# Stick-breaking heads with queries as rows and a scan over later keys

## The chip, the cores and the metric

The kernel runs on one core of one Trainium2 chip. The metric is device time in microseconds (us). Before the change three runs took 1114.95, 1115.48 and 1116.98 us, median 1115.48. One further execution was taken with the profiler; the profile and the trace below are of that one.

## The reference

The reference is a decoder of two layers, 512 tokens of width 1024 in fp32. Layer 0 has latent attention and differential attention, layer 1 has dilated attention and stick-breaking attention; a gated feed-forward part with a short convolution follows each. The change touches the four stick-breaking heads alone. For one head of width 64, with queries q, keys k and values v:

```python
strict = kpos[None, :] < qpos[:, None]
z = jnp.einsum('bhqd,bhkd->bhqk', qblk, k).astype(jnp.float32) * scale
log_beta = jax.nn.log_sigmoid(z)
log_keep = jnp.where(strict, jax.nn.log_sigmoid(-z), 0.0)
after = lax.cumsum(log_keep, axis=3, reverse=True) - log_keep
a = jnp.where(strict, jnp.exp(log_beta + after), 0.0)
return jnp.einsum('bhqk,bhkd->bhqd', a.astype(v.dtype), v)
```

With softplus(z) = log(1 + exp(z)), log_sigmoid(z) = z - softplus(z) and log_sigmoid(-z) = -softplus(z). So the weight of a key is exp(z - the sum of softplus over this key and all later keys in front of the query). That sum along the keys is what the change computes in another way.

## The kernel before, in words

TensorE does nearly all products of the layer's projections as three products each (`mm3`, L554 to L556): an fp32 operand is split into a part that is rounded to fp32r and its rest, and high times high, high times low and low times high are summed in PSUM. `split` (L461) makes the rounded part on ACT (L462) and the rest on DVE (L463). Weights go the same way: `Weights.load` brings a block of 128x1024 on SP's queue (L292) into one of three raw buffers, ACT casts it (L314), DVE makes the rest (L315), and up to five pairs are kept ahead of their use.

In the function `odd` (second layer) the token activations stand as `xh`, `xl`. `proj_T` computes a transposed projection of 128 columns by 512 tokens: 24 products into a bank named `apt`, which ACT (L1918) or DVE (L1920) then copies out. `proj_V` does the values by token blocks (`apv`, 24 narrower products for each block of 128 tokens), copied out to `sv` by ACT or DVE. Names of the PSUM banks used here: tag `a` has three banks, `s` two, `t`, `o` and `n` one each.

Four stick-breaking heads are worked as two pairs, u = 0 and u = 1; the heads of a pair lie in partitions 0 to 63 and 64 to 127 of `sq[u]` and `sk[u]`. Tokens are taken in four blocks of 128. Before the change a head's scores stand with keys as rows (partitions) and queries as columns: for key block j the queries from block j on, so 512 + 384 + 256 + 128 = 1280 columns, at the offsets `off`. For each pair:

- `sb_scores`: eight products (L1983) into `zp`, the two heads side by side; DVE adds the causal mask and writes `z` (L1987); DVE caps at 40 into `sp` (L1993); ACT takes exp (L1994).
- `sb_softplus`: ACT takes log of 1 + that (L1999), DVE takes the maximum with `z` (L2000). ACT loads its function table anew when it goes from exp to log and back.
- `sb_weights`: `sp` is split into `sh` (ACT) and `sl` (DVE). The sum over later keys runs over partitions, so TensorE does it: products with `tri`, whose first half holds -1 where a key is not earlier and whose second half is -1 throughout, add up the blocks j2 from j on, twice each (L2014, 20 products of 128 to 512 columns for each head, into `cp`). DVE adds `cp` to `z` (L2017), ACT takes exp of all 1280 columns (L2018).
- `sb_values`: eight products of `sv` with the weights, four for each head, into `osb` (L2024); `split` makes `oS` of it.

Between these steps stand eight `proj_T` for the dilated heads (`T12`), four for each pair, as work for TensorE while the other engines run. The order here is not written out by hand: the recorded order of the calls is passed to a list scheduler, which places instructions on each engine by its own costs. What follows (`score12`, first product L2090, and later) is again in hand-written order.

`store_sums(1, True)` (L426) has GpSimd's DMA queue add up some of the feed-forward weights in memory for later. Its first transfer is tied to the last DVE instruction that was written ahead of it.

Of the kernel before, what the change touches and what calls it, by code (L numbers as in the profile page):

```python
# [11 lines left out]
F32 = mybir.dt.float32  # L12
F32R = mybir.dt.float32r
BF16 = mybir.dt.bfloat16
AF = mybir.ActivationFunctionType
# [4 lines left out]
P = 128  # L20
# [329 lines left out]
def trunk(tc, A, out):  # L350
# [3 lines left out]
    with ExitStack() as top:  # L354
# [1529 lines left out]
        def odd(xnT, pending):  # L1884
            xh, xl = xnT
            with ExitStack() as es:
# [14 lines left out]
                                                                sb.tile([P, 2, S], F32, tag="sk", name="sk"))]  # L1901
                sv = sb.tile([P, NT, 256], F32, tag="sv", name="sv")
                smask = sb.tile([P, S], F32, tag="smask", name="smask")
                tri = sb.tile([P, 2, P], F32R, tag="tri", name="tri")
                trif = sb.tile([P, 2, P], F32, tag="z", name="trif", bufs=2)

                def proj_T(dst, scale, permuted, on_act):
                    acc = bank("a", "apt")
# [13 lines left out]
                def proj_V(dst, on_act=False):  # L1922
                    ws = [W.next() for _ in range(2)]

                    def tile_V(i):
                        t = slice(i * P, (i + 1) * P)
                        a = bank("a", "apv")
                        for k in range(KD):
                            wh, wl = ws[k // 4]
                            c = slice((k % 4) * 256, (k % 4 + 1) * 256)  # L1930
                            mm3(a[:, :256], xh[:, k, t], xl[:, k, t], wh[:, c], wl[:, c], k == 0, k == KD - 1)
                        if i % 2 and not on_act:
                            DVE.tensor_copy(dst[:, i], a[:, :256])
# [35 lines left out]
                tile_V = proj_V(sv)  # L1969
                for i in ORDER:  # L1970
                    tile_V(i)
                off = (0, 512, 896, 1152, 1280)
                spans = ((0, 0, 512), (1, 512, 896), (2, 896, 1280))

                def sb_scores(u):

                    zs = [sb.tile([P, 1280], F32, tag="z", name="z", bufs=2) for _ in range(2)]
                    for n, (j0, o0, o1) in enumerate(spans):
                        zp = [bank(t, "zp") for t in ("ss", "nt", "aa")[n]]
                        for j in (j0,) if j0 < 2 else (2, 3):  # L1980
                            for y in range(2):
                                r = slice(y * 64, y * 64 + 64)
                                PE.matmul(zp[y][:, off[j] - o0:off[j + 1] - o0], sk[u][r, j * P:(j + 1) * P],  # L1983
                                          sq[u][r, j * P:], start=True, stop=True)
                        for y in range(2):
                            for j in (j0,) if j0 < 2 else (2, 3):
                                DVE.tensor_tensor(zs[y][:, off[j]:off[j + 1]], zp[y][:, off[j] - o0:off[j + 1] - o0],  # L1987
                                                  smask[:, :S - j * P], ALU.add)

                    sps = []  # L1990
                    for z in zs:
                        sp = sb.tile([P, 1280], F32, tag="sp", name="sp", bufs=2)
                        DVE.tensor_scalar(sp[:], z[:], 40.0, None, ALU.min)  # L1993
                        ACT.activation(sp[:], sp[:], AF.Exp)  # L1994
                        sps.append(sp)
                    return list(zip(zs, sps))
# [3 lines left out]
                    DVE.tensor_tensor(sp[:], z[:], sp[:], ALU.max)  # L2000

                def sb_weights(z, sp):
                    sh = sb.tile([P, 1280], F32R, tag="sh", name="sh")
                    sl = sb.tile([P, 1280], F32R, tag="sl", name="sl")
                    split(sh[:], sl[:], sp[:])

                    for j0, o0, o1 in spans:
                        zp = bank("ssn"[j0], "cp")
                        for j in (j0,) if j0 < 2 else (2, 3):
                            n = S - j * P  # L2010
                            c = off[j] - o0
                            for j2 in range(j, NT):
                                for part in (sh, sl):
                                    PE.matmul(zp[:, c + (j2 - j) * P:c + n], tri[:, 0 if j2 == j else 1],  # L2014
                                              part[:, off[j2]:off[j2 + 1]], start=(j2 == j and part is sh),
                                              stop=(j2 == NT - 1 and part is sl))
                        DVE.tensor_tensor(z[:, o0:o1], z[:, o0:o1], zp[:, :o1 - o0], ALU.add)  # L2017
# [8 lines left out]

                T12 = [lambda t=t, x=x: proj_T(t[x], (-0.125, 1.0)[t is ck], True, t is cq)
                       for x in range(2, 6) for t in (cq, ck)]
                for u in range(2):
                    zs = sb_scores(u)  # L2030
                    for _ in range(2):
                        T12.pop(0)()
                    if u == 0:
                        with tc.manual_schedule(engines={POOL.engine}):
                            store_sums(1, True)
                    for v in zs:
                        sb_softplus(*v)
                    T12.pop(0)()
                    for v in zs:
                        sb_weights(*v)  # L2040
                    T12.pop(0)()
                    o = bank("o", "osb")
                    sb_values(u, [z for z, _ in zs], o)
# [276 lines left out]
def layout(inputs):  # L2320
# [76 lines left out]
    m = np.where(p < np.arange(P)[None, :], 0.0, -BIG)  # L2397
    o = np.zeros((P, P))
    r["sb_mask"] = np.concatenate([m, o, o, o], 1).astype(f)
    r["sb_tri"] = np.stack([-(p >= np.arange(P)[None, :]).astype(f), -np.ones((P, P), f)], 1)  # L2400
    return {k: np.ascontiguousarray(v) for k, v in r.items()}


# [13 lines left out]
```

## Time and profile before

| | before |
|---|---|
| median of three runs | 1115.48 us |
| profiled execution, its own time | 1116.25 us |
| its span, first to last instruction | 1114.5 us |
| PE (matmul) busy | 1104.3 us, 99% |
| DVE busy | 913.8 us, 82% |
| ACT busy | 638.6 us, 57% |
| granted TensorE clock, mean | 0.999 |

Engines are PE (TensorE's products), PEld (its weight loads), DVE (VectorE), ACT (ScalarE), POOL (GpSimd) and SP (SyncE, which here issues transfers). A row of a group names the line, the engine, the operation, output and inputs, the shape and the count, then the summed busy time and the mean of one in ns, then the idle time of the engine ahead of them with what ended it. A product that the program gives in fp32, as L1983 and L2024 are, appears as two records. The length of one product's record reaches beyond the start of the next, because products are pipelined; the time that a series takes is therefore read from start to start or from the chain of waits, which gives each piece's share of the path.

### The profile page before, as it was taken

Reading aid. Unit: us, or ns where it says so; the run is one execution under the profiler, and the core shown is the slowest. Engines: PE = TensorE matmul, PEld = TensorE weight load, DVE = VectorE, ACT = ScalarE, POOL = GpSimd, SP = SyncE. Lnnn points to the kernel's source line nnn. Section 1 sums busy time; section 2 is a strip of 40 time slices with the busy share of each in tenths; the row PEclk is TensorE's granted clock in tenths of the full one; section 3 lists DMA queues with packets and bytes.
Section 4 is the critical chain, followed back from the end, with each engine's and each line's share of the span. In section 5 each row is a group of like instructions: output and inputs, shape, how many; then the busy total and the mean of one; then the engine's idle time right before and its main releaser. Section 6 shows DMA issues by size and latency. Waiting matters only on the chain.

```text
span 1114.5 us, 17776 instructions
## 1 busy us (share of the span) xinstructions
PE 1104.3 (99%) x6556; PEld 951.7 (85%) x6556; DVE 913.8 (82%) x1628; ACT 638.6 (57%) x1127; POOL 219.1 (20%) x285
## 2 busy tenths in 40 slices
PE   9999999999999999999999999999999999999997
PEld 8766677898999999788888877788989999988886
DVE  5776687589999999999873565677899999999995
ACT  6554555447666666566553464654556676655662
POOL 2231022243022232000020030112521321220002
PEclk9999999999999999999999999999999999999999
DMA  8496122273444136455634295313534432265561
GB/s 309 161 216 109 54 95 96 76 248 124 152 137 157 42 101 251 137 174 178 233 110 169 78 244 132 97 53 112 192 129 154 144 123 76 78 250 180 159 213 76
DMA packets 53302, 162.14 MB, mean 145 GB/s; under 512 B 6720, under 2 KB 9184, under 8 KB 53216
## 3 DMA queue, kind: packets, MB, share of 16 engines
q1 hardware_dynamic: 45936, 145.22, 38.4%
q0 software_dynamic: 5312, 13.68, 6.4%
q10 hardware_dynamic: 1968, 2.12, 0.7%
q8 instruction: 51, 0.84, 0.3%
q14 instruction: 35, 0.29, 0.1%
HBM read 145.23 MB, written 27.28 MB: 155 GB/s over the span
## 4 chain that ended last, share of the span: by engine, by line
PE 92%; DVE 3%; DMA 2%; POOL 1%; issue 1%; ACT 0%; POOLq 0%; SPq 0%; DVEq 0%; ACTq 0%
PE u L554 13%; PE u L555 13%; PE u L556 13%; PE acc L555 6%; PE acc L556 6%; PE acc L554 6%; PE apt L554 3%; PE apt L555 3%; PE apt L556 3%; PE sps L1430 1%; PE ao L554 1%; PE ao L556 1%; PE ao L555 1%; PE aqk L1231 1%; PE aqk L1229 1%; PE aqk L1227 1%
## 5 line engine op out<-in xcount | busy, mean ns | idle before, releaser
L554 PE MATMUL u<-xh,wh 128*128 128x256 f32 (+1 forms) x664 | 212.3, 320 | 0.0
L555 PE MATMUL u<-xl,wh 128*128 128x256 f32 (+1 forms) x664 | 212.0, 319 | 0.0
L556 PE MATMUL u<-xh,wl 128*128 128x256 f32 (+1 forms) x664 | 211.6, 319 | 0.0
L732 DVE SCALAR_TENSOR_TENSOR y<-u,cw,y 128x511 f32<-128x511 f32 (+1 forms) x176 | 129.6, 746 | 9.2 <-ACT y L727 6.2
L315 DVE TENSOR_TENSOR wl<-wraw,wh 128x1024 fp32r<-128x1024 f32 x92 | 111.3, 1219 | 29.9 <-ACT wh L314 29.8
L556 PEld LDWEIGHTS u<-xh,wl 128*128 128x128 f32 x664 | 126.5, 190 | 9.0
L554 PEld LDWEIGHTS u<-xh,wh 128*128 128x128 f32 x664 | 126.6, 191 | 8.3
L555 PEld LDWEIGHTS u<-xl,wh 128*128 128x128 f32 x664 | 126.6, 191 | 8.0
L314 ACT CAST wh<-wraw 128x1024 fp32r<-128x1024 f32 x92 | 95.5, 1050 | 60.3 <-PE apt L555 18.0
L556 PE MATMUL u<-th,wl 128*128 128x256 f32 x416 | 117.7, 283 | 0.0
L555 PE MATMUL u<-tl,wh 128*128 128x256 f32 x416 | 117.7, 283 | 0.0
L554 PE MATMUL u<-th,wh 128*128 128x256 f32 x416 | 117.6, 283 | 0.0
L716 DVE TENSOR_TENSOR wl<-wraw,wh 128x512 fp32r<-128x512 f32 (+1 forms) x116 | 107.7, 938 | 2.2 <-ACT wh L864 1.5
L864 ACT CAST wh<-wraw 128x512 fp32r<-128x512 f32 (+1 forms) x104 | 86.5, 859 | 35.6 <-DVE wraw L851 23.0
L555 PE MATMUL acc<-wl,gh 128*128 128x512 f32 (+1 forms) x250 | 96.5, 389 | 0.1
L556 PE MATMUL acc<-wh,gl 128*128 128x512 f32 (+1 forms) x250 | 96.3, 388 | 0.0
L716 POOL TENSOR_TENSOR wl<-wraw,wh 128x512 fp32r<-128x512 f32 x48 | 62.3, 1298 | 172.0 <-issue 30.7
L554 PE MATMUL acc<-wh,gh 128*128 128x512 f32 (+1 forms) x250 | 93.6, 389 | 0.7 <-ACT wh L314 0.7
L727 ACT ACTIVATE y<-u,cw 128x512 f32<-128x512 f32 x88 | 67.5, 780 | 32.9 <-PE u L556 28.3
L554 PEld LDWEIGHTS u<-th,wh 128*128 128x128 f32 x416 | 79.8, 192 | 0.8
L555 PEld LDWEIGHTS u<-tl,wh 128*128 128x128 f32 x416 | 79.8, 192 | 0.7
L556 PEld LDWEIGHTS u<-th,wl 128*128 128x128 f32 x416 | 79.8, 192 | 0.0
(388 smaller groups left out, 2558.8 us busy)
## 6 DMA issues: line engine op xcount, KB each, us to landing
wraw<-in_ffn_w_up SPq DMA_DIRECT2D x82, 512.0 KB, 4.0
wraw<-in_ffn_w_down SPq DMA_DIRECT2D x44, 512.0 KB, 3.7
summed<-in_ffn_w_up POOLq DMA_DIRECT2D x24, 256.0 KB, 7.5
wraw<-summed SPq DMA_DIRECT2D x12, 512.0 KB, 4.2
wraw<-in_od_w_dqk SPq DMA_DIRECT2D x12, 512.0 KB, 3.9
wraw<-in_ffn_w_down SPq DMA_DIRECT2D x22, 256.0 KB, 3.2
wraw<-in_ev_w_dqk SPq DMA_DIRECT2D x8, 512.0 KB, 3.6
wraw<-in_ev_w_out SPq DMA_DIRECT2D x8, 512.0 KB, 3.6
```

What stands on the lines that cost most here:

```text
L314: self.nc.scalar.copy(h[:, :w], raw[:, :w])
L315: self.nc.vector.tensor_tensor(l[:, :w], raw[:, :w], h[:, :w].bitcast(F32), ALU.subtract)
L554: PE.matmul(o, lh, rh, start=first, stop=False, skip_group_check=more)
L555: PE.matmul(o, lh, rl, start=False, stop=False, skip_group_check=more)
L556: PE.matmul(o, ll, rh, start=False, stop=last, skip_group_check=more)
L716: return engine.tensor_tensor(o, a, b, ALU.subtract)
L727: ACT.activation(ys[n][:, z], us[n][z], AF.Identity, bias=cw[:, PAIRED[n], z, 3:4], scale=c[:, 2:3])
L732: DVE.scalar_tensor_tensor(y[:, z, d:], u[:, :S - d], c[:, 2 - d:3 - d], y[:, z, d:], ALU.mult, ALU.add)
L864: ACT.copy(ws[n][w][0][:, c], src)
L1227: PE.matmul(o, lh, rh, start=first, stop=False)
L1229: PE.matmul(o, lh, rl, start=False, stop=False)
L1231: PE.matmul(o, ll, rh, start=False, stop=last)
```

## The change

The heads' scores now stand with queries as rows and keys as columns: for query block i the keys up to block i, again 1280 columns in all, at the offsets `row`. The sum over later keys now runs along the columns, and DVE does it with a running scan: for each query block `tensor_tensor_scan` goes over the columns of `sp` from the last to the first (step -1), adds each to the sum so far, adds a zero (`none`, one column read again and again), and writes `kept` at the same reversed places. DVE subtracts `kept` from `z`. The value product needs keys as rows, so TensorE turns `z` block by block (ten transposes of 128x128 for each head, into `tz`), and ACT takes exp from the turned blocks in PSUM, three instructions in place of one, into `sp`. The triangle, its load and cast and the split of `sp` are gone. The mask is turned too.

The written order of the calls changes with it. The first pair's scores stand ahead of the value projection, which before stood in front of them. Of the eight projections in `T12`, two stand behind the first pair's softplus, one between its two heads' weights; then come the second pair's scores, ahead of the first pair's values; then two, one, one and one around the second pair's steps. `store_sums` is written behind the value projection.

```diff
-                tri = sb.tile([P, 2, P], F32R, tag="tri", name="tri")
-                trif = sb.tile([P, 2, P], F32, tag="z", name="trif", bufs=2)
+                none = sb.tile([P, 1], F32, tag="none", name="none")
...
-                nc.scalar.dma_start(trif[:], A["sb_tri"])
                 nc.scalar.dma_start(tab12[:], A["dil_tab12"])
-                DVE.tensor_copy(tri[:], trif[:])
+                DVE.memset(none[:], 0.0)
...
-                tile_V = proj_V(sv)
-                for i in ORDER:
-                    tile_V(i)
                 off = (0, 512, 896, 1152, 1280)
+                row = (0, 128, 384, 768, 1280)
...
-                    for n, (j0, o0, o1) in enumerate(spans):
+                    for n, at in enumerate((((3, 0),), ((2, 0), (0, 384)), ((1, 0),))):
                         zp = [bank(t, "zp") for t in ("ss", "nt", "aa")[n]]
-                        for j in (j0,) if j0 < 2 else (2, 3):
+                        for i, o in at:
                             for y in range(2):
                                 r = slice(y * 64, y * 64 + 64)
-                                PE.matmul(zp[y][:, off[j] - o0:off[j + 1] - o0], sk[u][r, j * P:(j + 1) * P],
-                                          sq[u][r, j * P:], start=True, stop=True)
+                                PE.matmul(zp[y][:, o:o + row[i + 1] - row[i]], sq[u][r, i * P:(i + 1) * P],
+                                          sk[u][r, :(i + 1) * P], start=True, stop=True)
...
                 def sb_weights(z, sp):
-                    sh = sb.tile([P, 1280], F32R, tag="sh", name="sh")
-                    sl = sb.tile([P, 1280], F32R, tag="sl", name="sl")
-                    split(sh[:], sl[:], sp[:])
+                    kept = sb.tile([P, 1280], F32, tag="sh", name="kept")
+                    for i in (3, 2, 1, 0):
+                        back = slice(row[i + 1] - 1, row[i] - 1 if i else None, -1)
+                        DVE.tensor_tensor_scan(kept[:, back], sp[:, back], none[:].to_broadcast([P, (i + 1) * P]), 0.0,
+                                               ALU.add, ALU.add)
+                    DVE.tensor_tensor(z[:], z[:], kept[:], ALU.subtract)
...
-                        zp = bank("ssn"[j0], "cp")
+                        tp = bank("ssn"[j0], "tz")
                         for j in (j0,) if j0 < 2 else (2, 3):
...
-                            for j2 in range(j, NT):
-                                for part in (sh, sl):
-                                    PE.matmul(zp[:, c + (j2 - j) * P:c + n], tri[:, 0 if j2 == j else 1],
-                                              part[:, off[j2]:off[j2 + 1]], start=(j2 == j and part is sh),
-                                              stop=(j2 == NT - 1 and part is sl))
-                        DVE.tensor_tensor(z[:, o0:o1], z[:, o0:o1], zp[:, :o1 - o0], ALU.add)
-                    ACT.activation(z[:], z[:], AF.Exp)
+                            for i in range(j, NT):
+                                c = off[j] - o0 + (i - j) * P
+                                PE.transpose(tp[:, c:c + P], z[:, row[i] + j * P:row[i] + (j + 1) * P], ident[:])
+                        ACT.activation(sp[:, o0:o1], tp[:, :o1 - o0], AF.Exp)
...
-                for u in range(2):
-                    zs = sb_scores(u)
...
+                def fill(n):
+                    for _ in range(n):
                         T12.pop(0)()
...
+                def finish(u, zs):
                     o = bank("o", "osb")
+                    sb_values(u, [sp for _, sp in zs], o)
                     split(oS[0][:, u], oS[1][:, u], o)
...
+                zs = sb_scores(0)
+                tile_V = proj_V(sv)
+                for i in ORDER:
+                    tile_V(i)
+                with tc.manual_schedule(engines={POOL.engine}):
+                    store_sums(1, True)
+                for v in zs:
+                    sb_softplus(*v)
+                fill(2)
+                sb_weights(*zs[0])
+                fill(1)
+                sb_weights(*zs[1])
+                first, zs = zs, sb_scores(1)
+                finish(0, first)
+                fill(2)
+                for v in zs:
+                    sb_softplus(*v)
+                fill(1)
+                sb_weights(*zs[0])
+                fill(1)
+                sb_weights(*zs[1])
+                fill(1)
+                finish(1, zs)
```

Line numbers of the changed kernel differ a little: there the scores are L1979, their mask L1983, the cap L1989, exp and log L1990 and L1995, the maximum L1996, the scan L2002 (listed as a scalar-tensor-tensor operation), the subtraction L2004, the transposes L2011, the exp L2012, the values L2018, the copies of a projection L1917 and L1919, those of `sv` L1932 and L1934, and the next part begins at L2099.

The order on PE in front of the last projections of the first pair, before (`apt` is a projection of `T12`, `cp` the sum over later keys, `sh` and `sl` the two parts of `sp`):

```order
L556 MATMUL apt<-xh,wl 128x512
L2014 MATMUL cp<-sh,tri 128x512
L2014 MATMUL cp<-sl,tri 128x512
L2014 MATMUL cp<-sh,tri 128x384
L2014 MATMUL cp<-sl,tri 128x384
L2014 MATMUL cp<-sh,tri 128x256
```

The same place on PE after the change (`tz` is the turned block):

```order
L556 MATMUL apt<-xh,wl 128x512
L2011 MATMUL tz<-ident,z 128x128 x10
L554 MATMUL apt<-xh,wh 128x512
L555 MATMUL apt<-xl,wh 128x512
L556 MATMUL apt<-xh,wl 128x512
```

The first five of a head's twenty products with the triangle are shown before; ten transposes in one series stand in their place, and the projections go on behind them.

PE where the second pair's scores are made, before, with buffer numbers (each number of `zp` is a bank; two numbers beside each other are the two heads):

```order
L2024 MATMUL osb_6748<-z_6497,sv_6027 64x128
L2024 MATMUL osb_6748<-z_6498,sv_6027 64x128
L1983 MATMUL zp_6761<-sq_6025,sk_6026 128x512
L1983 MATMUL zp_6762<-sq_6025,sk_6026 128x512
L1983 MATMUL zp_6767<-sq_6025,sk_6026 128x384
L1983 MATMUL zp_6768<-sq_6025,sk_6026 128x384
L1983 MATMUL zp_6773<-sq_6025,sk_6026 128x256
L1983 MATMUL zp_6774<-sq_6025,sk_6026 128x256
L1983 MATMUL zp_6773<-sq_6025,sk_6026 128x128
L1983 MATMUL zp_6774<-sq_6025,sk_6026 128x128
```

And after the change:

```order
L2011 MATMUL tz_6680<-ident_84,z_6380 128x128 x4
L2011 MATMUL tz_6686<-ident_84,z_6380 128x128 x3
L2011 MATMUL tz_6691<-ident_84,z_6380 128x128 x3
L1979 MATMUL zp_6705<-sk_6026,sq_6025 128x384
L1979 MATMUL zp_6705<-sk_6026,sq_6025 128x128
L1979 MATMUL zp_6698<-sk_6026,sq_6025 128x512
L1979 MATMUL zp_6699<-sk_6026,sq_6025 128x512
L1979 MATMUL zp_6704<-sk_6026,sq_6025 128x384
L1979 MATMUL zp_6704<-sk_6026,sq_6025 128x128
L1979 MATMUL zp_6714<-sk_6026,sq_6025 128x256
L1979 MATMUL zp_6715<-sk_6026,sq_6025 128x256
```

The scores stood behind the first pair's values (`osb`) and now stand ahead of them, directly behind the transposes of the first pair's second head. Banks 6698, 6699 and 6704 are those that `tz` 6680, 6686 and 6691 have just filled. The products of 384 and of 128 columns are no longer beside the other head's.

DVE in the second pair from the maximum on, before (`wl` is the rest of a weight block, `ck` a projection's copy):

```order
L2000 TENSOR_TENSOR sp<-z,sp 128x1280
L315 TENSOR_TENSOR wl<-wraw,wh 128x1024
L2000 TENSOR_TENSOR sp<-z,sp 128x1280
L463 TENSOR_TENSOR sl<-sp,sh 128x1280
L1920 TENSOR_SCALAR ck_6015<-apt 128x512
```

And after the change:

```order
L1996 TENSOR_TENSOR sp<-z,sp 128x1280
L1919 TENSOR_SCALAR ck_6014<-apt 128x512
L1996 TENSOR_TENSOR sp<-z,sp 128x1280
L315 TENSOR_TENSOR wl<-wraw,wh 128x1024
L2002 SCALAR_TENSOR_TENSOR kept<-sp,none 128x512
L2002 SCALAR_TENSOR_TENSOR kept<-sp,none 128x384
L2002 SCALAR_TENSOR_TENSOR kept<-sp,none 128x256
L2002 SCALAR_TENSOR_TENSOR kept<-sp,none 128x128
L2004 TENSOR_TENSOR z<-z,kept 128x1280
L315 TENSOR_TENSOR wl<-wraw,wh 128x1024
```

In place of the split stand four scans and a subtraction for the first head; the second head's follow the last row shown.

More of the change, by code (lines that the diff above doesn't have):

```diff
@@ L1977, in sb_scores @@
                     zs = [sb.tile([P, 1280], F32, tag="z", name="z", bufs=2) for _ in range(2)]
-                    for n, (j0, o0, o1) in enumerate(spans):
+                    for n, at in enumerate((((3, 0),), ((2, 0), (0, 384)), ((1, 0),))):
                         zp = [bank(t, "zp") for t in ("ss", "nt", "aa")[n]]
-                        for j in (j0,) if j0 < 2 else (2, 3):
+                        for i, o in at:
                             for y in range(2):
                                 r = slice(y * 64, y * 64 + 64)
-                                PE.matmul(zp[y][:, off[j] - o0:off[j + 1] - o0], sk[u][r, j * P:(j + 1) * P],
-                                          sq[u][r, j * P:], start=True, stop=True)
+                                PE.matmul(zp[y][:, o:o + row[i + 1] - row[i]], sq[u][r, i * P:(i + 1) * P],
+                                          sk[u][r, :(i + 1) * P], start=True, stop=True)
                         for y in range(2):
-                            for j in (j0,) if j0 < 2 else (2, 3):
-                                DVE.tensor_tensor(zs[y][:, off[j]:off[j + 1]], zp[y][:, off[j] - o0:off[j + 1] - o0],
-                                                  smask[:, :S - j * P], ALU.add)
+                            for i, o in at:
+                                DVE.tensor_tensor(zs[y][:, row[i]:row[i + 1]], zp[y][:, o:o + row[i + 1] - row[i]],
+                                                  smask[:, S - (i + 1) * P:], ALU.add)
                     sps = []
@@ L2002, in sb_weights @@
                 def sb_weights(z, sp):
-                    sh = sb.tile([P, 1280], F32R, tag="sh", name="sh")
-                    sl = sb.tile([P, 1280], F32R, tag="sl", name="sl")
-                    split(sh[:], sl[:], sp[:])
+                    kept = sb.tile([P, 1280], F32, tag="sh", name="kept")
[4 more added lines that the diff above has]
+                    DVE.tensor_tensor(z[:], z[:], kept[:], ALU.subtract)
                     for j0, o0, o1 in spans:
-                        zp = bank("ssn"[j0], "cp")
+                        tp = bank("ssn"[j0], "tz")
                         for j in (j0,) if j0 < 2 else (2, 3):
-                            n = S - j * P
-                            c = off[j] - o0
-                            for j2 in range(j, NT):
-                                for part in (sh, sl):
-                                    PE.matmul(zp[:, c + (j2 - j) * P:c + n], tri[:, 0 if j2 == j else 1],
-                                              part[:, off[j2]:off[j2 + 1]], start=(j2 == j and part is sh),
-                                              stop=(j2 == NT - 1 and part is sl))
-                        DVE.tensor_tensor(z[:, o0:o1], z[:, o0:o1], zp[:, :o1 - o0], ALU.add)
-                    ACT.activation(z[:], z[:], AF.Exp)
+                            for i in range(j, NT):
+                                c = off[j] - o0 + (i - j) * P
+                                PE.transpose(tp[:, c:c + P], z[:, row[i] + j * P:row[i] + (j + 1) * P], ident[:])
+                        ACT.activation(sp[:, o0:o1], tp[:, :o1 - o0], AF.Exp)
                 def sb_values(u, a, o):
@@ L2028, in odd @@
                        for x in range(2, 6) for t in (cq, ck)]
-                for u in range(2):
-                    zs = sb_scores(u)
-                    for _ in range(2):
+                def fill(n):
+                    for _ in range(n):
                         T12.pop(0)()
[L2033 to L2041, printed above, removed]
+                def finish(u, zs):
                     o = bank("o", "osb")
-                    sb_values(u, [z for z, _ in zs], o)
+                    sb_values(u, [sp for _, sp in zs], o)
                     split(oS[0][:, u], oS[1][:, u], o)
+                zs = sb_scores(0)
[21 more added lines that the diff above has]
+                finish(1, zs)
                 order = ExitStack()
@@ L2395, in layout @@
                                          for s in sl[g]], 1) for g, dl in ((1, 4), (2, 16))], 1).astype(f)
-    m = np.where(p < np.arange(P)[None, :], 0.0, -BIG)
+    m = np.where(np.arange(P)[None, :] < p, 0.0, -BIG)
     o = np.zeros((P, P))
-    r["sb_mask"] = np.concatenate([m, o, o, o], 1).astype(f)
-    r["sb_tri"] = np.stack([-(p >= np.arange(P)[None, :]).astype(f), -np.ones((P, P), f)], 1)
+    r["sb_mask"] = np.concatenate([o, o, o, m], 1).astype(f)
     return {k: np.ascontiguousarray(v) for k, v in r.items()}
```

## The prediction

> **What bounds the kernel now.** I read the page first: the engines' busy time.
>
> ```profile
> span 1114.5 us, 17776 instructions
> ## 1 busy us (share of the span) xinstructions
> PE 1104.3 (99%) x6556; PEld 951.7 (85%) x6556; DVE 913.8 (82%) x1628; ACT 638.6 (57%) x1127; POOL 219.1 (20%) x285
> ```
>
> TensorE is busy for 99% of the span, so time is won only where TensorE gets less to do, and lost wherever it is made to wait. Second came the chain of waits over the second layer (columns: start, length, engine and line). It runs on TensorE through all of the stick-breaking part:
>
> ```profile
> 622.33 2.36 PE zp L1983 x16
> 641.26 2.70 PE cp L2014 x20
> 645.40 0.59 PE cp L2014 x3
> 646.93 2.26 PE cp L2014 x17
> 652.43 2.30 PE osb L2024 x16
> 654.74 2.36 PE zp L1983 x16
> 673.69 2.70 PE cp L2014 x20
> 677.84 0.59 PE cp L2014 x3
> 679.36 2.26 PE cp L2014 x17
> 684.87 2.30 PE osb L2024 x16
> 687.17 1.09 PE z L2090 x16
> 693.93 1.09 PE z L2090 x16
> ...
> 740.99 1.89 PE t L2116 x16
> ...
> 761.52 0.87 PE tp L502 x8
> ```
>
> Between these pieces stand the three-product projections (`apt`), back to back. The two pairs of heads (u = 0 and 1) are alike. Third, the windows of the value projection `sv`, of the two pairs and of the last feed-forward part (columns: window, its length, busy us of PE, PEld, DVE, ACT, POOL, granted clock, DMA share, GB/s):
>
> ```profile
> 610.60:622.30 11.70, 11.70 (x99) 11.53 (x98) 3.06 (x5) 2.47 (x3) 0.00 (x0) 1.00 0.15 46
> 622.30:652.40 30.10, 30.10 (x155) 24.60 (x154) 20.06 (x26) 19.19 (x19) 7.24 (x13) 1.00 0.56 171
> 652.40:684.80 32.40, 32.40 (x170) 25.64 (x169) 20.61 (x27) 17.82 (x17) 7.11 (x8) 1.00 0.95 199
> ...
> 780.00:1114.00 334.00, 327.96 (x2028) 296.07 (x2026) 306.16 (x441) 200.00 (x301) 66.41 (x53) 1.00 0.44 148
> ```
>
> In the first three rows PE has no gap and a granted clock of 1.00; DVE and ACT have about a third of the time free. The question is therefore: how much PE work goes, and does DVE still deliver in time.
>
> **The change, part by part.** The order of the instructions at the three places that follow stands with the change above. *Products with the triangle go.* On PE, twenty products for each head are replaced by ten transposes. The products stand on the path with 2.70 + 0.59 + 2.26 = 5.55 us for each pair: **-11.10 us**. A transpose of a 128x128 fp32 block is in the chain at L502: 8 in 0.87, 0.109 each, so 40 take **+4.35 us**. Bounds: the 16 small products of L2090 in 1.09 (0.068 each) give 2.7, the 16 of L2116 in 1.89 (0.118) give 4.7. I take L502, the same operation between the same neighbours.
>
> *The projections are cut elsewhere.* Now: 72 in one piece from 624.69 to 641.26 = 16.57, then 24 in three pieces of 1.44, 0.94 and 3.24 = 5.62; for both pairs 44.4. An uncut block of 24 takes 693.93 - 688.26 = 5.67. After: blocks of 48, 24, 72, 24, 24, which by these two rows take 11.12 + 5.67 + 16.57 + 5.67 + 5.67 = 44.7: **+0.3**. The value projection moves behind the first scores with equal neighbours: nothing.
>
> *The second pair's scores* move ahead of the first pair's values, right behind the transposes. Before, each size stood as two neighbours, one for each head. The row of the widest size shows that such neighbours overlap (eight records of 641 ns fill 2.3 us, not 5.1):
>
> ```profile
> L1983 PE MATMUL zp<-sq,sk 64*128 64x512 f32 x8 | 2.3, 641 | 0.0
> ...
> L1918 ACT ACTIVATE cq<-apt 128x512 f32<-128x512 f32 x4 | 2.3, 584 | 0.0
> ```
>
> With the change 384 and 128 of the two heads are apart. Of the 2.36 us of a whole score step, 512 of 1280 columns have 0.94; that much is lost if nothing overlaps. In addition `zp_6698`, `zp_6699` and `zp_6704` need the banks that the three exps empty, and ACT does a 0.58 cast-out of `cq` first: 0.58 + 0.58 + two of 384 columns, by estimate 0.13 shorter each (as DVE's rows of 512 and 384 below) = 2.1 us from the last projection on, of which the transposes hide 1.09. Bounds: 0, and 0.94 + 1.0 = 1.9 us. The wait and the lost overlap fall at the same place and partly cover each other: **+0.9**.
>
> Sum: -11.10 + 4.35 + 0.3 + 0.9 = **-5.55 us**, if no other wait appears.
>
> *The scan.* No scan is in the trace. Four instructions at L2002 are one head's scans; S is the time of the four. Rows that bound S:
>
> ```profile
> L2017 DVE TENSOR_TENSOR z<-z,cp 128x512 f32<-128x512 f32 x4 | 2.7, 683 | 2.7 <-PE cp L2014 2.7
> L2017 DVE TENSOR_TENSOR z<-z,cp 128x384 f32<-128x384 f32 x8 | 4.2, 550 | 0.0
> L1987 DVE TENSOR_TENSOR z<-zp,smask 128x256 f32<-128x256 f32 x4 | 1.6, 412 | 0.0
> L1987 DVE TENSOR_TENSOR z<-zp,smask 128x128 f32<-128x128 f32 x4 | 1.1, 278 | 0.0
> L2071 DVE RECIPROCAL share<-share 128x4 f32<-128x4 f32 x4 | 0.7, 178 | 0.1
> L2071 DVE RECIPROCAL share<-share 128x16 f32<-128x16 f32 x1 | 0.3, 253 | 0.0
> ```
>
> At an add's pace S = 0.68 + 0.55 + 0.41 + 0.28 = 1.9 us. The slowest row for each element is the reciprocal: 75 ns more for 12 elements, 6.25 each, so 1280 would take 8.0, with four starts of 0.15 S = 8.6. [...] I take S nearer to the adds, 2 to 4. [...]
>
> Does DVE deliver? Rows of the second pair now:
>
> ```profile
> 656.01 3.26 DVE L1987 TENSOR_TENSOR z<-zp,smask 128x512 f32<-128x512 f32 x8
> 659.20 1.69 DVE L1993 TENSOR_SCALAR sp<-z 128x1280 f32<-128x1280 f32 x2
> ...
> 660.18 2.44 ACT L1994 ACTIVATE sp<-sp 128x1280 f32<-128x1280 f32 x2 [4.80 <-DVE sp L1993]
> 662.63 1.28 ACT L1999 ACT_TABLE_LOAD   x1
> 663.93 1.27 ACT L1999 ACTIVATE sp<-sp 128x1280 f32<-128x1280 f32 x1
> ...
> 666.64 1.22 DVE L315 TENSOR_TENSOR wl<-wraw,wh 128x1024 fp32r<-128x1024 f32 x1
> 667.83 1.49 DVE L2000 TENSOR_TENSOR sp<-z,sp 128x1280 f32<-128x1280 f32 x1
> ...
> 670.64 0.68 DVE L1920 TENSOR_SCALAR ck<-apt 128x512 f32<-128x512 f32 x1
> ```
>
> After the change `sp` holds the weights that the first pair's value products read, so the second pair's chain begins when these end (E). First logarithm done: E + 0.85 + 2.44 + 1.28 + 1.27 = E + 5.8. Then DVE: two maxima, `ck`, a weight's rest = 4.9; scan S; subtraction 1.49: transposes ready at E + 12.2 + S. PE comes to them after 72 projections, at E + 16.6. Cover gone at S = 4.4. The second head needs another rest (1.22), S and 1.49: E + 14.9 + 2S, against E + 16.6 + 1.1 + 5.7 = E + 23.3: S = 4.2. In the first pair, from its scores (Z): PE comes to the second head's transposes at Z + 2.4 + 11.7 + 11.1 + 1.1 + 5.7 = Z + 32.0. DVE: the first scores 0.9, a rest and the adds 4.5, then as above 5.8 to the logarithm, two maxima 3.0, a copy of `sv` an estimated 0.4 (the adds' 256 columns), two rests 2.4, two subtractions 3.0: Z + 20.0 + 2S, so S = 6.0. The waits are 2S - 8.4 and 2S - 12.0, where positive.
>
> *Cost nothing:* the removed casts `sh`, rests `sl`, adds of `cp`, the load and cast of the triangle, and the twelve exps from PSUM in place of four; ACT and DVE work that S and these rows leave inside the third that is free. The POOL sums of L426 are tied to the last DVE instruction written ahead of them, `ck` before, now a copy of `sv`:
>
> ```profile
> 638.92 3.72 POOL L426 DMA_DIRECT2D summed<-in_ffn_w_up  x7 [62.55 <-DVE ck L1920]
> ```
>
> The copy stands between the first pair's maxima, at Z + 12.7 with Z = 622.3 - 11.7 = 610.6: 623.3, 15 us sooner. There they lie over more weight loads (columns: KB, median us to landing; before and from 638):
>
> ```profile
> wraw<-in_od_w_dqk SPq DMA_DIRECT2D x9, 512.0 KB, 3.6
> ```
>
> ```profile
> wraw<-in_od_w_dqk SPq DMA_DIRECT2D x3, 512.0 KB, 7.7
> ```
>
> Nine loads ahead of the sums landed in 3.6 us, three under them in 7.7, and PE had no gap even then: a load is issued when one of three buffers is free, and each weight feeds 5.5 us of PE. On SP the table for the later heads now stands ahead of the output weights and waits for the last scan's buffer, free at least 9 us before the next scores; nothing.
>
> **Rivals.** (1) *Slow scan, slower than before.* From S = 4.2 PE waits at the transposes; from S = 6.5 (4.6 + 1.0 = 5.6) the gain is gone; at the reciprocal's pace, S = 8.6, the waits are 8.8 + 5.2 = 14.0, net +8.4: 1123.9 against the median. For: no scan in the trace, reversed columns, and both bounds of S lie astride 4.2. Against: the streaming rows agree on 1.05 ns an element, and 4.2 is more than twice that. Chance 0.10, of which 0.06 beyond 6.5. (2) *Given back later.* In the last 334 us DVE is busy for 306 and PE idles 6; if DVE or a load that is not tied to this part sets the end there, nothing is gained: 1115.5. Against: the work there starts from this layer's output, and the chain is PE's until then. Chance 0.07. (3) *Bank waits at full price*, and transposes at L2116's: -11.10 + 4.7 + 0.3 + 1.9 = -4.2: 1111.3. Chance 0.15; still faster.
>
> **How the numbers follow.** The profiled execution took 1116.25 (span 1114.5 and 1.75 around it), 0.77 above the median 1115.48. 1116.25 - 5.55 = 1110.7, or 1109.9 against the median. The forecast without a new wait has 0.68. Its own bounds are 2.7 us for the transposes without any lost overlap (-8.1, 1107.4) and -4.2 (1111.3); the range leaves out the rare lowest end and reaches up to S near 5 (a wait of 1.6: 1111.5) and the spread of the runs, 1114.95 to 1116.98: 1107.8 to 1112.8. A difference of 0.2%, 2.2 us, is about what a measurement can tell. Faster by more: 0.68 + 0.15 + 0.03 of the slow scan = 0.86; within: 0.07 + 0.01 = 0.08; slower: 0.06.
>
> **What would show it.** Right: chain pieces `tz` of about 1.1 us four times, no `cp`; the distance from the first score piece to the first L2099 piece, less the 11.7 us of value projection that now lies within, falls from 64.8 to about 59.3. Wrong: a gap on PE ended by DVE's L2004 (scan rows above 2 us at 512 columns), the second score step beyond 3.3 us with ACT as its releaser, or the same distance shorter while the end is not.

## The result, and the profile after

| | before | after |
|---|---|---|
| median of the runs taken side by side | 1116.63 us (5 runs) | 1110.82 us (5 runs, 1109.03 to 1111.85) |
| profiled execution, its own time | 1116.25 us | 1110.82 us |
| its span | 1114.5 us | 1109.0 us |

The ratio is 0.995, interval 0.9936 to 0.9965: a small gain, but clear of the noise. It is 5.8 us between the medians and 5.5 us between the profiled spans; 5.55 us were forecast. The first lines of the page after:

```profile
span 1109.0 us, 17705 instructions
## 1 busy us (share of the span) xinstructions
PE 1098.6 (99%) x6516; PEld 946.0 (85%) x6516; DVE 918.1 (83%) x1632; ACT 633.9 (57%) x1131; POOL 219.2 (20%) x285
```

PE is busy 5.7 us less and is still the bound; DVE took on 4.3 us. The chain of waits after, over the same part of the layer as was shown of before:

```profile
610.84 2.36 PE zp L1979 x16
635.82 1.09 PE tz L2011 x10
642.41 1.09 PE tz L2011 x10
643.50 3.22 PE zp L1979 x14
646.73 2.30 PE osb L2018 x16
665.62 1.09 PE tz L2011 x10
672.21 1.09 PE tz L2011 x10
678.80 2.30 PE osb L2018 x16
681.10 1.09 PE z L2099 x16
...
709.09 4.26 DMA stat<-swap
...
717.11 1.47 PE z L2151 x8
```

Where `cp` stood with 2.70, 0.59 and 2.26 us stand `tz` pieces of 1.09, and no engine but PE is in the chain up to L2099: PE does not wait for the scan. From the first score piece to the first L2099 piece it is 681.10 - 610.84 = 70.26 us. Before it was 687.17 - 622.33 = 64.84, and 11.6 more of value projection (610.65 to 622.25, from start to start), which now lies within: 76.4. This distance, called the stage below, fell by 6.2 us; the span fell by 5.5. Of the 0.7 us between them, the stage starts 0.1 later, and the pieces at the end of the fence belong to the other 0.6. The second score piece, 3.22 against 2.36, is a term of the prediction; both come back below.

The scan, which no trace had shown, in the groups of the stage (by shape; the order listing calls it SCALAR_TENSOR_TENSOR, the profile TENSOR_TENSOR_SCAN):

```profile
L2002 DVE TENSOR_TENSOR_SCAN kept<-sp,none 128x512 f32<-128x512 f32 x4 | 4.9, 1219 | 0.0
...
L2002 DVE TENSOR_TENSOR_SCAN kept<-sp,none 128x128 f32<-128x128 f32 x4 | 1.6, 403 | 0.0
...
L2004 DVE TENSOR_TENSOR z<-z,kept 128x1280 f32<-128x1280 f32 x4 | 6.0, 1491 | 0.1
```

And in DVE's timeline of the second pair, where four scans in a row are merged (start, length, then the idle time ahead where there is any):

```profile
659.58 2.96 DVE L2002 TENSOR_TENSOR_SCAN kept<-sp,none 128x512 f32<-128x512 f32 x4
662.58 1.49 DVE L2004 TENSOR_TENSOR z<-z,kept 128x1280 f32<-128x1280 f32 x1
...
668.12 1.49 DVE L2004 TENSOR_TENSOR z<-z,kept 128x1280 f32<-128x1280 f32 x1
```

One head's scans take S = 2.96 us. The first head's subtraction ends at 662.58 + 1.49 = 664.07, and PE comes to its transposes at 665.5: a cover of 1.4 us. The second head's ends at 669.61, PE comes at 672.05: 2.4. In the first pair the same reading gives 3.5 and 5.6 us.

### The profile page after: what moved, and what is told of

It is laid out like the page before. It is cut to its first block, busy times and chain, and to the rows that moved or that the text cites. A ratio compares the mean times of both kernels' runs of the same rounds, so it can differ in the third digit from the quotient of the medians.

```text
span 1109.0 us, 17705 instructions
## 1 busy us (share of the span) xinstructions
PE 1098.6 (99%) x6516; PEld 946.0 (85%) x6516; DVE 918.1 (83%) x1632; ACT 633.9 (57%) x1131; POOL 219.2 (20%) x285
## 2 busy tenths in 40 slices
DMA packets 53158, 162.01 MB, mean 146 GB/s; under 512 B 6704, under 2 KB 9040, under 8 KB 53072
```

## The experiments

The theory: the gain is PE work that is gone (-11.10 of products, +4.2 of transposes, +0.86 in the second scores), and the new order of the calls only keeps the scan behind PE's projections. The rivals: the order itself brings the gain; the scan costs something on the path; the second scores wait for banks and not for lost overlap; something is given back later. Since the program ahead of the stage differs by up to 2.7 us from one execution to the next (the first scores start at 609.5 to 612.2 in these traces with the same code ahead), small effects are read from the stage and not from the end. The stage is the distance defined above, read from each run's chain; where the values' projection stands ahead of it, 11.6 us are added (with three scans, where the chain leaves PE, the start of the first score's record was taken).

| kernel | stage, us | its time, us |
|---|---|---|
| before | 76.4 | 1116.4 (16 runs) |
| old arithmetic, new order | 76.5 | 1115.9 (10 runs) |
| new arithmetic, old order | 79.7 | 1119.2 (5 runs) |
| after, and once more | 70.3, 70.5 | 1110.8, 1111.2 (5 runs each) |
| scores paired | 69.4 | 1109.5 (5 runs) |
| each transpose twice | 73.8 | 1114.8 (1 run) |
| each scan twice, three times | 76.7, 90.0 | 1117.4, 1129.5 (1 run each) |
| scan forward | 70.3 | 1108.9 (1 run) |
| no scan; with late sums | 71.5; 70.2 | 1112.7; 1109.1 (1 run each) |
| late sums | 70.2 | 1110.3 (1 run) |

**The arithmetic and the order apart.** The first kernel keeps the products with the triangle in the new order of calls. Against the changed kernel, in part (the scores, the mask and the triangle are those of before as well):

```diff
...
-                    DVE.tensor_tensor(z[:], z[:], kept[:], ALU.subtract)
+                    sh = sb.tile([P, 1280], F32R, tag="sh", name="sh")
+                    sl = sb.tile([P, 1280], F32R, tag="sl", name="sl")
+                    split(sh[:], sl[:], sp[:])
...
```

> The arithmetic, the layout and the triangle's products of the kernel before, written in the new order of calls (value projection behind the first scores, the heads' weights apart, fills of 2, 1, 2, 1, 1, 1). Theory (the gain is TensorE work that is gone, and the new order only keeps the scan off the path): the PE work is the one before, 11.1 us of cp and no tz, and PE never waited before, so nothing is won: 1116.0 to 1117.5 beside 1116.6 of before, the twenty cp products of each pair back in the chain. Rival 'the order brings the gain, not the products': about 1111, as the changed kernel.

Measured: 1115.93 us, ratio to before 1.0001 (0.9992 to 1.001). Its chain has the old pieces back:

```profile
612.18 2.36 PE zp L1981 x16
...
637.16 2.70 PE cp L2012 x20
...
647.51 0.61 DVE z L2015
648.16 2.89 PE zp L1981 x14
...
669.90 2.70 PE cp L2012 x20
678.14 2.70 PE cp L2012 x20
...
688.67 1.09 PE z L2103 x16
```

The order alone brings nothing. The expectation took it that PE would not wait; it does, and two small terms cancel. The projections, in fewer pieces, take 44.0 us in place of 44.4, read from start to start. The second scores, now behind the triangle's products, wait 0.5 us in all for DVE's additions, which empty their banks, and take 2.8 in place of 2.4.

The second kernel is the other half, the new arithmetic in the order of before (in part; the value projection stands in front again):

```diff
...
-                sb_weights(*zs[0])
-                fill(1)
-                sb_weights(*zs[1])
...
+                    for v in zs:
+                        sb_weights(*v)
+                    fill(1)
...
```

> The new arithmetic (scan, transposes, queries as rows) in the old order of calls: value projection first, both heads' weights one behind the other, fills of 2, 1, 1 for each pair. Theory (products bring the gain, order keeps the scan off the path): PE comes to the second head's transposes 1.1 us behind the first's, but DVE needs a scan and a subtraction more, 2.97 + 1.49 = 4.5 us, so PE waits about 3.4 us in each pair, and some 1 to 2 us more where the first head's cover (measured: 3.5 and 1.4 us) went with the 11.7 us of value projection: 6 to 8 us of waits ended by DVE's L2004 rows against 5.5 won, 1116.5 to 1119.5, not faster than before. Rival 'the products alone decide, the order is of no account': 1111, no wait. Rival 'the order alone': 1116.6, no wait.

Measured: 1119.19 us, ratio 1.003 (1.0018 to 1.0042): slower than before, with the same PE work as the changed kernel. Its waits and its chain:

```profile
PE tz L2014 <- DVE z L2007: 7.9, 4, 2.7
```

```profile
670.28 1.45 DVE kept L2005 x2
...
675.34 2.98 DVE kept L2005 x4
678.34 1.50 DVE z L2007
679.98 2.37 PE tz L2014 x10
```

PE waits 7.9 us in four places for the subtraction behind the scan; DVE is in the chain where PE was. So the products are the gain, and the order is what lets it be kept: the change is worth 5.5 us with it and costs 3 us without it. Both rivals of this kind fall.

**How much the scan may cost.** Each scan is issued two, then three times (shown for two):

```diff
-                        DVE.tensor_tensor_scan(kept[:, back], sp[:, back], none[:].to_broadcast([P, (i + 1) * P]), 0.0,
-                                               ALU.add, ALU.add)
+                        for _ in range(2):
+                            DVE.tensor_tensor_scan(kept[:, back], sp[:, back], none[:].to_broadcast([P, (i + 1) * P]), 0.0,
+                                                   ALU.add, ALU.add)
```

> The changed kernel with each scan issued twice (same result): a head's scans take 5.94 us in place of 2.97. Theory (the scan lies beside PE's projections with measured covers of 3.5 and 5.6 us in the first pair, 1.4 and 2.4 in the second): first pair nothing or 0.3 at the second head, second pair waits of 2.97 - 1.4 = 1.6 and 5.94 - 2.4 - 1.6 = 2.0 us, ended by DVE's subtraction; sum 3.9, up to 6.5 if weights' rests (1.22 each) that the order now puts between the doubled scans fall into it: 1114.7 to 1117.3. By the formula of the prediction, 2S - 8.4 = 3.5. Rival 'the scan is on the path': 4 x 2.97 = 11.9 more, 1122.7. Rival 'DVE's time is of no account here': 1110.8, no wait.

> The changed kernel with each scan issued three times: 8.9 us for each head, 5.94 more. Theory: by the same covers the waits are 2.4 and 3.8 us in the first pair, 4.5 and 4.9 in the second, 15.7 together, up to 18.5 with rests in between: 1126.5 to 1129.3; so the third issue costs all of its 11.9 us, where the second cost only about 4 to 6. Rival 'on the path': 2 x 11.9 = 23.8 more, 1134.6. Rival 'of no account': 1110.8.

Measured: the stage is 6.4 us longer with two, 13.3 more with the third; 1117.41 and 1129.47 us, each 0.1 to 0.2 above the range that was expected. The waits of PE, first with two and then with three scans:

```profile
PE tz L2012 <- DVE z L2005: 5.4, 3, 2.7
```

```profile
PE tz L2012 <- DVE z L2005: 13.1, 4, 5.0
```

The second issue adds 11.9 us to DVE and about half of it to the path, at three of the four places; the third adds another 11.9 and costs all of it and more. It is the cover that decides, as the formula said, though the formula's 3.5 us at S = 5.94 was too low: the rests of weights that the scheduler now put between the scans lie on DVE's way too, and there is a cost of a wait that no term had. The windows of the kernel with two scans, across its longest wait (columns as before):

```profile
664.00:666.00 2.00, 2.00 (x10) 1.68 (x9) 2.00 (x4) 0.00 (x0) 0.00 (x0) 1.00 1.02 265
666.00:668.00 2.00, 0.66 (x3) 0.20 (x2) 1.97 (x4) 1.20 (x2) 0.00 (x0) 1.00 0.59 119
668.00:669.30 1.30, 0.00 (x0) 0.00 (x0) 1.29 (x1) 1.12 (x1) 0.00 (x0) 0.75 0.46 101
669.30:671.40 2.10, 2.06 (x11) 2.06 (x11) 2.08 (x3) 0.86 (x2) 0.00 (x0) 0.50 0.50 195
```

PE stands still for 2.7 us, the granted clock falls to 0.50, and the ten transposes behind it take 2.05 us in place of 1.01. The length of the wait alone does not decide it: in the kernel with the old order one wait of 2.7 us cost no clock (1.00 behind it) and a later one of 2.4, shortly behind one of 1.8, did: the granted clock was 0.50 there, and the ten transposes took 2.37 in its chain.

**The scan taken away.** Here DVE subtracts each score's own term, and the sums over later keys are left out (the lines of the scan go too):

```diff
...
-                    DVE.tensor_tensor(z[:], z[:], kept[:], ALU.subtract)
+                    DVE.tensor_tensor(z[:], z[:], sp[:], ALU.subtract)
```

> The changed kernel without its scans: each score has its own term subtracted in place of the sum over its later keys, so the sums are left out and 4 x 2.97 us of DVE work go. Theory (the scan costs nothing, as PE never waits for DVE in this stage): the stage from the first score piece to the first L2099 piece stays 70.3 us, give or take 0.3, the second score step at 3.2; time within the runs of the changed kernel, 1109.0 to 1111.9. Rival 'part of the scan is on the path': the stage shorter by what of the 11.9 us is not covered, at most to the 1.4 us of the smallest cover.

Measured: a miss. The stage is longer, 71.50 us, with 11.9 us less for DVE to do. All of the 1.2 us is in the second score step. Its waits:

```profile
PEld zp L1979 <- ACT sp L2007: 1.2, 1, 1.2
PE zp L1979 <- ACT sp L2007: 1.0, 1, 1.0
```

and ACT's timeline ahead of it:

```profile
639.71 1.05 ACT L314 CAST wh<-wraw 128x1024 fp32r<-128x1024 f32 x1 [6.64 <-DMA wraw<-in_od_w_dqk]
640.78 1.28 ACT L2007 ACT_TABLE_LOAD   x1
...
644.84 1.04 ACT L314 CAST wh<-wraw 128x1024 fp32r<-128x1024 f32 x1 [1.41 <-PE tz L2006]
645.79 0.59 ACT L1917 ACTIVATE cq<-apt 128x512 f32<-128x512 f32 x1
646.28 1.35 ACT L2007 ACTIVATE sp<-tz 128x512 f32<-128x512 f32 x3
```

That is the bank wait that the prediction priced: PE wants to write the second scores at 644.8, and the exps that empty their banks begin at 646.3, behind a cast of a weight block that is itself late. The view puts this cast's wait down to PE's transposes, but the load that it reads was issued at 630.47 and landed only at 644.77, 14.3 us later and just ahead of the cast. A guess at the reason was that POOL's sums slow the weight loads (from 625 to 648 us five loads have a median of 10.3 us to landing, in the changed kernel 9.6); with DVE faster, buffers come free sooner, and three loads are issued under the sums by 633.9, where the changed kernel issues its third at 637.8. The next kernel moves only the wait of POOL's first DMA, from the copy of `sv` to DVE's work behind the second scores:

```diff
-                with tc.manual_schedule(engines={POOL.engine}):
-                    store_sums(1, True)
...
                 first, zs = zs, sb_scores(1)
+                with tc.manual_schedule(engines={POOL.engine}):
+                    store_sums(1, True)
```

> The kernel without scans (it leaves the sums over later keys out), with one thing more: POOL's sums of L426 are written behind the second pair's scores, so that their first DMA waits for the adds of these scores (about 648) and not for the copy of sv (625.7); the order of the instructions is the same on every engine. Theory (without scans DVE gave back its weight buffers earlier, so two weight loads were issued under POOL's sums and landed late, the cast and with it the exps that empty the banks of the second scores came late, and PE waited 1.3 us): with the sums gone from that time the casts are not late, no wait of PE for ACT at the second scores, their step 3.2 in place of 4.5, the stage 70.2 in place of 71.5. Rival 'the exps come late for a reason of ACT's own order': the step stays at 4.5.

Measured: the sums start at 649.9, the stage is 70.21, the step 3.22, and PE waits for ACT nowhere. ACT at the same place:

```profile
641.10 1.05 ACT L314 CAST wh<-wraw 128x1024 fp32r<-128x1024 f32 x1 [2.87 <-PE apt L555]
642.05 0.59 ACT L1917 ACTIVATE cq<-apt 128x512 f32<-128x512 f32 x1
642.54 1.35 ACT L2007 ACTIVATE sp<-tz 128x512 f32<-128x512 f32 x3
```

Relative to the first scores (612.18 there, 609.73 here) the exps come 1.3 us earlier, and no cast waits for a load: the weight loads at this place land after 3.5 to 5.1 us, under the sums it was 8 to 14. So the miss was not the scan: POOL's sums, by way of a late weight load, a late cast and late exps, held up PE. And with the wait gone, the scan's absence moves the stage by nothing (70.21 against 70.26): the scan is wholly hidden.

The changed kernel itself with the sums moved in the same way:

> The changed kernel with POOL's sums of L426 written behind the second pair's scores (first DMA at about 648 in place of 624.4); the order of the instructions is the same on every engine. Theory: at the second scores nothing is gained (3.2 stays, as the changed kernel had no bank wait in one execution and 0.3 in the other); the cast that waited 5.6 us for a weight load no longer waits; in the second pair the loads now lie under the sums, and there DVE's cover is only 1.4 us: a wait of PE for DVE's subtraction of 0 to 2 us, stage 70.2 to 72.3. Rival 'the sums cost nothing wherever they lie': 70.2, no new wait.

Measured: stage 70.24, second step 3.22, no wait of PE in the second pair: the fear that the loads under the sums would eat the 1.4 us there was unfounded. Where the sums lie costs the changed kernel nothing, or as little as in its second execution, next.

**The second scores.** The changed kernel was run once more, and beside it one with the second pair's scores in another order and other banks:

```diff
-                    for n, at in enumerate((((3, 0),), ((2, 0), (0, 384)), ((1, 0),))):
-                        zp = [bank(t, "zp") for t in ("ss", "nt", "aa")[n]]
+                    for n, at in enumerate(((((3, 0),), ((2, 0), (0, 384)), ((1, 0),)),
+                                            (((2, 0), (0, 384)), ((1, 0),), ((3, 0),)))[u]):
+                        zp = [bank(t, "zp") for t in (("ss", "nt", "aa"), ("aa", "at", "ss"))[u][n]]
```

> The changed kernel once more, on the chip of the three others, to set them beside it: 1110.8, distance from the first score piece to the first L2099 piece 70.3 us (58.6 without the values' 11.6), second score step 3.2, and, if it is of the order of the queues and not chance, the wait of DVE for the swap of the statistics near 714 us (2.25 us) again.

> The changed kernel, with the second pair's scores in the order 384 + 128, 256, 512 and in other banks, so that the products of 384 columns of the two heads stand as neighbours again and no bank of an exp is needed early. Theory (the 0.86 us that the second score step takes more than the first is lost overlap of the two heads' products): second zp piece 2.3 to 2.4 us in place of 3.22, the stage 0.9 shorter, 1109.9 beside 1110.8. Rival 'the 0.86 is the wait for the banks that the exps empty': as the banks go too, this kernel alone would look the same, but then its products of 384 columns keep 495 ns each and the step before would show ACT as the releaser in the changed kernel. Rival 'given back later': the step shorter, the end the same.

Measured for the repeat: 1111.17 us, ratio 0.9955 (0.9941 to 0.9968); its second score step takes 3.5 us, 0.2 to 0.3 of it a wait of PE's weight load for ACT's exp:

```profile
PEld zp L1979 <- ACT sp L2012: 0.2, 1, 0.2
```

For the new order: 1109.48 us, ratio 0.9942 (0.9929 to 0.9954). Its chain:

```profile
610.09 2.36 PE zp L1980 x16
...
642.75 2.36 PE zp L1980 x16
...
679.45 1.09 PE z L2100 x16
```

The step is 2.36 again, the stage 69.36, 0.9 below the changed kernel. In the executions where PE waits for no one at this step (the changed kernel, late sums, forward scan) it takes 3.22 each time. The records of the changed kernel show the same: from 643.43 to 644.29 one head's products of 384 and 128 columns start alone, before any of the other head. So 0.86 is the overlap of the two heads that is lost when one head's 384 and 128 columns go first, and what comes on top (0.3 in the repeat, 1.3 without scans) is the bank wait. The new order takes both away. It is the fastest of the kernels that keep the sums over later keys; its interval overlaps that of the changed kernel, and what tells them apart is the stage.

**The transposes' price.**

```diff
-                                PE.transpose(tp[:, c:c + P], z[:, row[i] + j * P:row[i] + (j + 1) * P], ident[:])
+                                for _ in range(2):
+                                    PE.transpose(tp[:, c:c + P], z[:, row[i] + j * P:row[i] + (j + 1) * P], ident[:])
```

> The changed kernel with each of the 40 transposes issued twice (same result). Theory (transposes stand on PE's path, back to back, at 0.109 us): 40 x 0.109 = 4.4 more, less up to 0.7 if the second score step then finds its banks free and its heads in step: 1114.5 to 1115.2; pieces tz of 2.1 us in place of 1.0. Rival 'transposes hide in waits for banks or cost as L2116': 0 or 4.7 more.

Measured: 1114.81 us, stage 73.79. Its chain:

```profile
636.92 2.18 PE tz L2012 x20
...
644.57 2.18 PE tz L2012 x20
646.75 2.51 PE zp L1979 x14
```

Four times 1.09 more is 4.36, and the second score step gives back 0.7: its products stand there in another order, 512 columns first and the two heads side by side for each size, and they take 2.51 in place of 3.22. That makes 3.6, measured 3.5, and the step tells once more that the heads' order is what costs 0.86.

**The reversed columns.**

```diff
-                        back = slice(row[i + 1] - 1, row[i] - 1 if i else None, -1)
+                        back = slice(row[i], row[i + 1])
```

> The changed kernel with the scans over columns in rising order; it sums the earlier keys in place of the later ones, all else the same. Theory (the scan's pace, 2.1 ns for an element, is the hand-over of the sum, not the reversed addresses): rows of 1.22 us at 512 columns as before, time 1110.8. Rival 'the reversed columns halve the pace': rows of about 0.68 us at 512 columns, S = 1.9, and the same time, as the scan is hidden.

Measured: the stage is 70.26, and the scan's group reads

```profile
L2002 DVE TENSOR_TENSOR_SCAN kept<-sp,none 128x512 f32<-128x512 f32 x4 | 4.9, 1220 | 0.0
```

1220 ns against 1219: the step of -1 costs nothing, and the scan's pace is not that of the reversed columns. Why an element takes 2.1 ns is not shown by it, nor by another run; the hand-over of the sum was the author's assumption.

## Why the prediction was right, point by point

- *Bound and products.* The forecast's frame held: PE without a gap, so what leaves PE leaves the time. -11.10 us is what went; the kernel with the old arithmetic in the new order puts it back. The distance that was to fall from 64.8 to about 59.3 fell to 58.6 (70.26 without the 11.6 of value projection).
- *Transposes.* +4.35 forecast, +4.2 from start to start (1.01, 1.18, 1.01, 1.01), and 1.09 for ten in the chain; doubling them shows that the price stands on the path. The row of L502 was the right one to take.
- *Projections cut elsewhere.* +0.3 forecast, -0.15 measured (44.25 for 44.40). The term was mis-sized, by 0.45: the block of 48 took 10.91, not 11.12, and an uncut block of 24 between transposes 5.58, not the 5.67 of the row that was used.
- *Second scores.* +0.9 forecast, +0.86 measured, but not as it was worked out. It was to be a bank wait and lost overlap that partly cover each other; in the profiled execution it was lost overlap alone, and the two add up: 0.86 + 0.3 in the repeat. That the number fits so well is luck. In the repeat the step's 3.5 us, with ACT as the releaser of a part, passes the 3.3 that were named as a sign of being wrong, though the time stays in the range. The upper bound of 1.9 was passed without scans (0.86 + 1.3 = 2.2).
- *The scan.* S was taken as 2 to 4, and is 2.96. Its slope, (1219 - 403) / 384 = 2.1 ns an element, with 403 ns for 128 columns, is twice the adds' 1.05 and a third of the reciprocal's 6.25. So the choice of a pace nearer to the adds held, though no run shows what sets it. The formula left 4.4 - 2.96 = 1.4 for the first head of the second pair, and 1.4 was measured. For the second head it left (8.4 - 5.9) = 2.5, measured 2.4. The first pair's second head, 6.1 by formula, has 5.6.
- *Slow scan, as a rival.* It did not come true, but its mechanism is real: with two scans for one PE waits at the transposes. In the second pair the waits are 2.7 + 1.15 = 3.8 us, where the formula gives 3.5; in the first pair it gives none, and 1.55 were measured at the second head, where a weight's rest stands among the scans. Behind the longest wait the price is more than the wait, since the granted clock is 0.50 there (ten transposes 2.05 us in place of 1.01).
- *Nothing for the sums that start 15 us sooner.* They did (624.40). "PE had no gap even then" held for the weight loads as such, but the argument missed a second way: a late load makes ACT's cast late, the cast stands ahead of the exps, and the exps free the banks of the second scores. Its price was 0 in the profiled execution, 0.3 in the repeat, and 1.3 where DVE ran ahead.
- *Given back later.* 6.2 us were won in the stage and 5.5 at the end. 0.1 is the stage's later start, and 0.6 lies at 713 to 718: DVE waits 2.3 us, before it was 0.8, for the swap of the statistics (a 16 KB transfer on GpSimd's queue), which the chain above shows with 4.26 us, and PE's L2151 piece takes 1.47 in place of 1.06. The transfer's time to landing, in the row of the changed kernel and that of its repeat:

```profile
stat<-swap POOLq DMA_DIRECT2D x1, 16.0 KB, 4.3
```

```profile
stat<-swap POOLq DMA_DIRECT2D x1, 16.0 KB, 2.9
```

Issued at the same place, it lands after 2.8 to 3.1 us in nine of the thirteen profiled executions, that of before among them, and after 4.3 to 4.6 in four. It differs between two executions of one kernel, so it is no consequence of the change; why it comes in two lengths was not tried and stays open.

The sum of the measured terms is -11.10 + 4.21 - 0.15 + 0.86 = -6.18, with 0.6 given back by that transfer and 0.1 later at the start of the stage: -5.5. So the forecast of -5.55 is nearer than its terms were, and that is luck: a term 0.45 too high, and a transfer that it did not have, nearly cancel.

## What to carry to other kernels

Where one engine has no gap, a step can move to an engine that is half free, but only with the cover worked out for each head and with the order of the calls changed to supply it: the same arithmetic was worth -5.5 us with its order and +3 without it. When a queue's work is moved, follow it beyond the engine that reads it: load, cast, the exps behind the cast, the banks they free. And read small terms from a stage, from start to start, when the program ahead of it varies by more than they are worth.

## What the runs showed of the hardware

- A running scan on DVE costs 2.1 ns an element, twice an add's 1.05, and has the same price forward and backward (1220 and 1219 ns for 512 columns).
- Behind a wait of PE of 2.7 us (two scans), and behind one of 2.4 shortly after one of 1.8 (old order), the granted clock of TensorE was 0.50 for the next 2 us (ten transposes 2.05 us in place of 1.01, and in the chain of the other 2.37 in place of 1.09); behind another wait of 2.7 us (old order) it was 1.00.
- Products of 64 rows for two heads overlapped where the heads alternated with equal shapes: 16 pieces in 2.36 us, and 3.22 where one head's 384 and 128 columns went first, with the same shapes in all.
- A weight load of 512 KB landed after 3.6 us ahead of POOL's sums (median of nine, before); under them the medians were 7.7 (three, before), 9.6 (five, changed kernel) and 10.3 us (five, no scan), and one cast waited 5.6 us for such a load in the changed kernel, 6.6 without scans.
